# A two-layer decoder trunk on one core: the pacing of weight tiles that are split ahead of their use

## The chip, the cores and the metric

The kernel runs on one core of a Trainium2 chip. The metric is the device time of one execution in microseconds. The kernel before takes 1213.51 us, the median of three runs (1212.63 to 1216.22). Its profiled execution took 1216.67 us, of which the span from the first to the last instruction is 1214.9 us.

## The reference, cut to what matters

The input is 512 tokens of 1024 channels in float32. Two layers follow each other. Each normalises the input, projects it, runs four token mixers side by side, projects their outputs back and adds them. Then comes a feed-forward stage, and it is in the first layer's feed-forward stage that the change works:

```
h = rms_norm(x, ffn_norm[l])
g, up = jnp.split(h @ w_ffn_in[l], 2, axis=-1)      # 1024 -> 2 x 2816
x = x + (jax.nn.silu(g) * up) @ w_ffn_out[l]        # 2816 -> 1024
```

A last normalisation follows the second layer.

## The kernel before, in words

**Split products.** Every float32 matrix product is made of three matmuls in fp32r (`mm3`, L424). A weight tile of 128 x 512 numbers (256 KB) is loaded as `raw`. ScalarE (ACT) rounds it to `whi`, and VectorE (DVE), or now and then GpSimd (POOL), forms `wlo = raw - whi` (`load_split`, L522 to 532). Activations are split in the same way. TensorE (PE) then adds whi*xhi, whi*xlo and wlo*xhi into one PSUM tile. A weight tile holds four blocks of 128 columns, so it feeds 12 matmuls.

**The feed-forward stage** (L1191 to 1241). The 22 tiles of 128 hidden units are taken in two halves of 11. In a half, each hidden tile has a gate product and an up product (`dense_fm`, 24 matmuls each). DVE evicts them from PSUM as `fg` and `fu`, with the factor `rbc` of the normalisation. ACT applies silu to `fg`, DVE multiplies the two, and the result is split into `hsh` (ACT) and `hsl` (DVE or POOL). After 11 such tiles the half's output product follows: 8 output tiles of 33 matmuls each, added to `x` by DVE. So a half is 528 matmuls on `w_gu` and 264 on `w_fo`. In layer 0, 98 of the first 528 stand ahead of the small matmuls `ps_rbc` of the normalisation in PE's order; in layer 1 it is 95.

**Tiles split ahead.** During layer 0's feed-forward stage, the weights of layer 1's mixers are split ahead (`split_ahead`, L495). Such a tile is loaded as `praw`, ACT rounds it to `phi`, DVE or POOL forms `plo`, and both are written to device memory as `ahead`. When layer 1 needs the tile, it loads the two halves and casts nothing (L511 to 521). There are 64 such tiles, 54 of 256 KB and 10 of 128 KB. L1196 gives each of the 22 hidden tiles an equal share of them, and gates the share behind the last matmul of that hidden tile's gate product. The two output products get none.

**The order.** Nothing runs in the order of the source. Every instruction is recorded with an engine, a cost and a priority. A planner (`schedule`, L244) then plays a machine of five engines through and puts down each engine's instructions in the order in which it started them. Each engine executes its own list strictly in that order, and waits where an operand isn't there. Tiles split ahead have the lowest priority (60, `P_AHEAD`), evictions 2 and loads 1. At most two `praw` buffers and four `pre` buffers (`phi` and `plo`) exist at a time (`LIMIT`, L51).

**How the planner reckons a load.** L199 and L357 to 360: the DMA starts 0.7 us after the issuing instruction, which costs 0.48 us. It moves 360 GB/s, which makes 0.73 us for 256 KB, and its landing is seen 0.3 us later. So a 256 KB load with nothing ahead of it is reckoned to be there 2.2 us after its issue begins. All DMAs are issued by SyncE (SP), in its own list's order.

Of the kernel before, what the change touches and what calls it, by code (L numbers as in the profile page):

```python
# [23 lines left out]
KT = D // P  # L24
QT = S // P
HID = 2816
HT = HID // P
HH = HT // 2
# [80 lines left out]

class Op:  # L110
    __slots__ = ("i", "eng", "fn", "args", "kw", "cost", "tail", "table", "prio", "preds", "succs", "bufs", "news",
                 "left", "est", "far", "start", "end", "idle", "flex", "lock")


FLEXIBLE = ("tensor_sub", "tensor_mul", "tensor_add")
# [17 lines left out]
class Recorder:  # L133
# [55 lines left out]
    def add(self, eng, method, args, kw):  # L189
        op = Op()  # L190
        op.i = len(self.ops)
        op.eng, op.fn, op.args, op.kw = eng.name, getattr(eng.nc_engine, method), args, kw
        writes = [args[0]] + ([kw["accum_out"]] if "accum_out" in kw else [])
        writes = [w for w in writes if isinstance(w, View)]
        reads = [a for a in (*args[1:], *(v for k, v in kw.items() if k != "accum_out")) if isinstance(a, View)]
        views = writes + reads
        op.cost = self.cost(eng.name, method, args, kw, views) / self.share + self.extra
        op.tail = 0.0
        if method == "dma_start":  # L199
            op.tail = views[0].cols * 4 * P / 360.0  # L200
        op.flex = None
        if eng.name == "dve" and method in FLEXIBLE and not any(v.buf.cls == "psum" for v in views):
            op.flex = getattr(self.pool.nc_engine, method), self.cost("pool", method, args, kw, views)
        op.lock = (method in ("tensor_sub", "tensor_mul", "tensor_add") and eng.name == "pool" and "op" not in kw
                   or eng.name == "dve" and method not in ("memset", "reciprocal")
                   and not any(v.buf.cls == "psum" for v in views))
        op.idle = 0.0
        if method == "matmul":
            l, r = args[1:3]
            op.idle = op.cost - (4 if r.dtype == F32 else 1) * r.cols / 2.4 * (l.p[1] - l.p[0]) / P  # L210
        op.table = TABLES.get(args[2]) if method == "activation" else None
        op.prio = self.prio
        preds = set(self.gate)
        op.bufs = []
        for vs, w in ((writes, True), (reads, False)):
            for v in vs:
                b = v.buf
                if b not in op.bufs:
                    op.bufs.append(b)
                if b.cls == "psum":  # L220
                    if b.log:
                        preds.add(b.log[-1])
                    b.log = [op.i]
                    continue
                p0, p1, m = v.region()
                keep = []
                for e in b.log:
                    j, jw, q0, q1, k = e
                    hit = p0 < q1 and q0 < p1 and (m & k)
                    if hit and (w or jw) and j != op.i:  # L230
                        preds.add(j)
                    if not (w and hit and p0 <= q0 and q1 <= p1 and (m & k) == k and j != op.i):
                        keep.append(e)
                keep.append((op.i, w, p0, p1, m))
                b.log = keep
        preds.discard(op.i)
        op.bufs += [v.buf for v in self.also if v.buf not in op.bufs]
        for b in op.bufs:
            b.uses += 1
        op.preds, op.succs = preds, []  # L240
        self.ops.append(op)
        return op

    def schedule(self):  # L244
# [49 lines left out]
        while done < len(ops):  # L294
# [8 lines left out]
            for e in engines:  # L303
                fu, re = future[e], ready[e]
                while fu and fu[0][0] <= t:
                    _, i = heapq.heappop(fu)
                    heapq.heappush(re, (ops[i].prio, i))
                if busy[e] > t or not re:
                    continue
                skipped, pick = [], None  # L310
                while re:
                    c = heapq.heappop(re)
                    op = ops[c[1]]
                    if op.start is not None:
                        continue
                    if e == "pool" and op.flex and busy["dve"] + SPILL * len(ready["dve"]) < t + op.flex[1]:
                        skipped.append(c)
                        continue
                    if e == "pe":
                        late = op.prio > -5.0 and (t < op.far or (op.idle > 0.4 * op.cost and cool > COOL)) and (re or skipped)  # L320
                    else:
                        late = e == "act" and op.table not in (None, table) and t - op.est < 5000.0 and (re or skipped)
                    if not late and place(op):
                        pick = op
                        break
                    skipped.append(c)
                    if len(skipped) > 60:
                        break
                if pick is None and e in ("pe", "act"):
                    for c in skipped:  # L330
                        if place(ops[c[1]]):
                            pick = ops[c[1]]
                            skipped.remove(c)
                            break
                for c in skipped:
                    heapq.heappush(re, c)
                if pick is None:
                    continue
                op = pick
                if e != op.eng:  # L340
                    op.eng, (op.fn, op.cost) = e, op.flex
                cost = op.cost * (2 if e == "pe" and t < WARM else 1 if e == "pe" else CARE)
                if op.table and op.table != table:
                    cost += 1300.0
                    table = op.table
                if e == "pe":
                    cool = max(0.0, cool + op.idle + t - busy[e] - 0.5 * (cost - op.idle))
                if op.lock:
                    other = held["pool" if e == "dve" else "dve"]
                    cost = max(cost, other - t + cost - 145.0)  # L350
                    held[e] = t + cost
                op.start, op.end = t, t + cost
                busy[e] = op.end
                order.append(op)
                done += 1
                moved = True
                if op.tail:  # L357
                    dma = max(dma, op.end + 700.0) + op.tail
                    op.tail = dma + 300.0 - op.end
                fin = op.end + op.tail  # L360
                for b in op.bufs:
                    b.uses -= 1
                    if not b.uses:
                        heapq.heappush(frees, (fin + RELEASE, op.i, b.n, b))
                for j in op.succs:
                    s = ops[j]
                    lat = LATENCY[e][s.eng] + (0.0 if s.eng == e else SLACK if s.eng == "pe" else SPARE)
                    s.est = max(s.est, fin + lat)
                    if s.eng != e:
                        s.far = max(s.far, fin + lat)  # L370
                    s.left -= 1
                    if not s.left:
                        heapq.heappush(future[s.eng], (s.est, s.i))
                        if s.flex:
                            heapq.heappush(future["pool"], (s.est, s.i))
# [25 lines left out]
def trunk_kernel(ctx: ExitStack, tc: tile.TileContext, io):  # L401
    nc = tc.nc
    R = Recorder(nc)
# [91 lines left out]
    def split_ahead(key, ap):  # L495

        n = ap.shape[-1]
        raw = t512("praw", F32, "praw", (n,))
        sp.dma_start(raw, ap)
        hi, lo = t512("pre", F32R, "phi", (n,)), t512("pre", F32R, "plo", (n,))  # L500
        with also(lo):
            act.copy(hi, raw)
# [616 lines left out]
    for l in range(L):  # L1119
# [68 lines left out]
        fnrm = nrm  # L1188
        last = l == L - 1
        later = [] if last else mixer_weights(l + 1)  # L1190
        for half in range(2):  # L1191
            hs = []
            for m in range(half * HH, (half + 1) * HH):
                pg = dense_fm(io["w_gu"][l, m, 0], fnrm)
                with prio(P_AHEAD), gate(R.ops[-1]):
                    for key, ap in later[m * len(later) // HT:(m + 1) * len(later) // HT]:  # L1196
                        split_ahead(key, ap)
                g = scaled(pg, fnrm, "fg", group="h")
                pu = dense_fm(io["w_gu"][l, m, 1], fnrm)
                with prio(P_EVICT):  # L1200
# [9 lines left out]
            with prio(P_DENSE):  # L1210
                w = Weights(io["w_fo"][l, half])
                for m in range(KT - tail):
                    ps = psum("d", "pd")
                    for k in range(HH):
                        end = mm3(ps, w.block(m * HH + k), hs[k], k == 0, k == HH - 1)
                    if m < KT - 1:
                        turn["w"] = end
                    with prio(P_NORM):
# [131 lines left out]
```

## Time and profile before

| | |
|---|---|
| median of three runs | 1213.51 us |
| profiled execution | 1216.67 us |
| its span | 1214.9 us |
| PE busy | 1176.7 us, 97% of the span |
| DVE, ACT, POOL busy | 57%, 44%, 18% |
| DMA moved | 175.26 MB, mean 144 GB/s |

All arithmetic stands on L397 of the profile, which is the line that emits the planned instructions. So the rows are told apart by the names of their tiles, not by lines. The stages of layer 0's feed-forward lie between 242 and 625 us, those of layer 1 between 842 and 1206 us. Matmuls are pipelined: each is shown some 390 ns long, and the next one starts some 227 ns after it.

### The profile page before, as it was taken

Reading aid. Unit: us, or ns where it says so; the run is one execution under the profiler, and the core shown is the slowest. Engines: PE = TensorE matmul, PEld = TensorE weight load, DVE = VectorE, ACT = ScalarE, POOL = GpSimd, SP = SyncE. Lnnn points to the kernel's source line nnn. Section 1 sums busy time; section 2 is a strip of 40 time slices with the busy share of each in tenths; the row PEclk is TensorE's granted clock in tenths of the full one; section 3 lists DMA queues with packets and bytes.
Section 4 is the critical chain, followed back from the end, with each engine's and each line's share of the span. In section 5 each row is a group of like instructions: output and inputs, shape, how many; then the busy total and the mean of one; then the engine's idle time right before and its main releaser. Section 6 shows DMA issues by size and latency. Waiting matters only on the chain.

```text
span 1214.9 us, 16334 instructions
## 1 busy us (share of the span) xinstructions
PE 1176.7 (97%) x5552; PEld 963.5 (79%) x5552; DVE 686.5 (57%) x1270; ACT 532.2 (44%) x971; POOL 219.1 (18%) x208
## 2 busy tenths in 40 slices
PE   8999989999989999989999999999999999999996
PEld 6778768788767888767888787888888888888886
DVE  7668778777555355455433575587544533544433
ACT  5546967554433234344323348555333322333331
POOL 5423453272000000000112312204300000000010
PEclk9999989999999999999999999999999999999998
DMA  6312132268877357777476423643333333222312
GB/s 204 118 44 74 54 113 70 69 217 295 260 256 232 100 185 268 236 237 244 140 215 216 126 86 119 229 137 121 104 96 98 99 99 96 96 96 96 102 55 70
DMA packets 101651, 175.26 MB, mean 144 GB/s; under 512 B 11328, under 2 KB 21952, under 8 KB 101568
## 3 DMA queue, kind: packets, MB, share of 16 engines
q1 hardware_dynamic: 101568, 174.22, 45.0%
q8 instruction: 44, 0.72, 0.2%
q14 instruction: 39, 0.32, 0.1%
HBM read 139.04 MB, written 35.13 MB: 143 GB/s over the span
## 4 chain that ended last, share of the span: by engine, by line
PE 58%; DMA 7%; DVE 1%; ACT 1%; issue 1%; SPq 1%; POOL 0%; DVEq 0%; ACTq 0%; POOLq 0%
PE pd L397 49%; PE pt L397 4%; DMA praw<-w_outa 3%; DMA praw<-w_tm 2%; PE ps_s L397 1%; DMA ahead<-phi 1%; ACT phi L397 1%; PE ps_o L397 1%; PE ps_pt L397 1%; SPq L397 1%; DMA praw<-w_outb 1%; DMA ahead<-plo 1%; PE ps_q L397 0%; PE ps_og L397 0%; DVE plo L397 0%
## 5 line engine op out<-in xcount | busy, mean ns | idle before, releaser
L397 PE MATMUL pd<-xhi,whi 128*128 128x512 f32 x896 | 351.5, 394 | 14.3 <-DVE fg L397 6.6
L397 PE MATMUL pd<-xhi,wlo 128*128 128x512 f32 x896 | 350.5, 393 | 0.7 <-POOL wlo L397 0.7
L397 PE MATMUL pd<-xlo,whi 128*128 128x512 f32 x896 | 351.1, 393 | 0.0
L397 ACT CAST whi<-raw 128x512 fp32r<-128x512 f32 (+2 forms) x330 | 200.9, 612 | 327.9 <-PE pd L397 283.8
L397 DVE TENSOR_TENSOR wlo<-raw,whi 128x512 fp32r<-128x512 f32 (+1 forms) x276 | 201.6, 733 | 163.4 <-ACT whi L397 150.8
L397 PEld LDWEIGHTS pd<-xhi,whi 128*128 128x128 f32 x896 | 168.6, 188 | 54.9 <-ACT whi L397 15.4
L397 PEld LDWEIGHTS pd<-xhi,wlo 128*128 128x128 f32 x896 | 168.1, 188 | 36.7 <-POOL wlo L397 1.7
L397 PEld LDWEIGHTS pd<-xlo,whi 128*128 128x128 f32 x896 | 168.7, 188 | 35.0 <-issue 1.4
L397 PE MATMUL pd<-hsh,whi 128*128 128x512 f32 (+1 forms) x374 | 142.1, 380 | 4.6 <-ACT hsh L397 4.1
L397 PE MATMUL pd<-hsl,whi 128*128 128x512 f32 (+1 forms) x374 | 141.8, 379 | 0.3 <-DVE hsl L397 0.3
L397 PE MATMUL pd<-hsh,wlo 128*128 128x512 f32 (+1 forms) x374 | 141.5, 378 | 0.0
L397 POOL TENSOR_TENSOR wlo<-raw,whi 128x512 fp32r<-128x512 f32 (+2 forms) x54 | 69.7, 1292 | 303.3 <-ACT whi L397 287.3
L397 POOL TENSOR_TENSOR sq<-sq 128x512 f32<-128x512 f32 x35 | 51.1, 1459 | 375.1 <-ACT sq L397 367.4
L397 PEld LDWEIGHTS pd<-hsh,whi 128*128 128x128 f32 x374 | 70.8, 189 | 18.7 <-ACT hsh L397 4.9
L397 DVE TENSOR_TENSOR plo<-praw,phi 128x512 fp32r<-128x512 f32 (+1 forms) x53 | 36.6, 693 | 80.9 <-ACT phi L397 80.9
L397 ACT CAST phi<-praw 128x512 fp32r<-128x512 f32 (+1 forms) x64 | 37.4, 587 | 102.2 <-DMA praw<-w_tm 23.0
L397 PEld LDWEIGHTS pd<-hsl,whi 128*128 128x128 f32 x374 | 70.7, 189 | 14.0 <-DVE hsl L397 1.0
L397 PEld LDWEIGHTS pd<-hsh,wlo 128*128 128x128 f32 x374 | 70.7, 189 | 12.8
L397 DVE TENSOR_TENSOR x<-x,pd 128x512 f32<-128x512 f32 (+1 forms) x66 | 43.3, 669 | 54.2 <-PE pd L397 54.1
L397 PE MATMUL pt<-whi,xlo 128*128 128x512 f32 x128 | 51.0, 398 | 0.0
L397 PE MATMUL pt<-whi,xhi 128*128 128x512 f32 x128 | 50.7, 396 | 0.0
L397 PE MATMUL pt<-wlo,xhi 128*128 128x512 f32 x128 | 50.6, 396 | 0.0
(259 smaller groups left out, 1523.9 us busy)
## 6 DMA issues: line engine op xcount, KB each, us to landing
raw<-w_gu SPq DMA_DIRECT2D x176, 256.0 KB, 2.6
raw<-w_fo SPq DMA_DIRECT2D x88, 256.0 KB, 2.7
ahead<-phi SPq DMA_DIRECT2D x54, 256.0 KB, 2.6
ahead<-plo SPq DMA_DIRECT2D x54, 256.0 KB, 3.4
whi<-ahead SPq DMA_DIRECT2D x54, 256.0 KB, 2.7
wlo<-ahead SPq DMA_DIRECT2D x54, 256.0 KB, 3.1
x<-xT SPq DMA_DIRECT2D x16, 256.0 KB, 5.4
raw<-w_fm SPq DMA_DIRECT2D x16, 256.0 KB, 2.6
```

The lines of the kernel that those rows point to most:

```text
L397: op.fn(*[r(a) for a in op.args], **{k: r(v) for k, v in op.kw.items()})
```

## The change

It has two parts. First, the 64 tiles are paced by matmuls done, over both gate-up halves and both output products. `pace(n)` is called after each gate product (n = 16) and after each output tile (n = 11). It releases tiles until the share released equals the share of the stage's 528 block steps that are behind. Second, the planner reckons that what waits for a `praw` load gets it 3.5 us later than before (`slow`). The reckoned occupancy of the DMA engines is not changed, and neither are other loads or the writes of `ahead`.

```
-        op.tail = 0.0
+        op.tail, op.slow = 0.0, 0.0
...
-                    op.tail = dma + 300.0 - op.end
+                    op.tail = dma + 300.0 + op.slow - op.end
...
-        sp.dma_start(raw, ap)
+        sp.dma_start(raw, ap).slow = 3500.0
...
+        total, paced = len(later), [0]
+        def pace(n):
+            paced[0] += n
+            with prio(P_AHEAD), gate(R.ops[-1]):
+                while later and (total - len(later)) * HT * 3 * KT < paced[0] * total:
+                    split_ahead(*later.pop(0))
...
-                with prio(P_AHEAD), gate(R.ops[-1]):
-                    for key, ap in later[m * len(later) // HT:(m + 1) * len(later) // HT]:
-                        split_ahead(key, ap)
+                pace(2 * KT)
...
+                    pace(HH)
```

PE's list is the same before and after, instruction by instruction. What moves stands on the other engines.

**Place 1.** ACT's list at the silu of the first half's tenth hidden tile (`fg_3861` before, `fg_3792` after). The number behind a name tells buffers apart. Before:

```order
L397 CAST phi_3774<-praw_3750 128x512
L397 CAST whi_3780<-raw_3725 128x512
L397 CAST phi_3788<-praw_3759 128x512
L397 CAST whi_3805<-raw_3744 128x512
L397 CAST hsh_3828<-fu_3808 128x512
L397 CAST whi_3833<-raw_3769 128x512
L397 CAST phi_3843<-praw_3816 128x512
L397 CAST whi_3856<-raw_3803 128x512
L397 ACTIVATE fg_3861<-fg_3861 128x512
```

and after:

```order
L397 CAST whi_3719<-raw_3667 128x512
L397 CAST whi_3740<-raw_3689 128x512
L397 CAST phi_3746<-praw_3699 128x512
L397 CAST phi_3753<-praw_3703 128x512
L397 CAST hsh_3761<-fu_3738 128x512
L397 CAST whi_3768<-raw_3713 128x512
L397 CAST whi_3794<-raw_3731 128x512
L397 ACTIVATE fg_3792<-fg_3792 128x512
```

Before, `phi_3843` is the last cast but one ahead of the silu, and it stands ahead of the cast of `raw_3803`, a load that SP issued before `praw_3816`. After, the `phi` casts come in pairs, four `whi` casts apart, and `phi_3746` stands behind the cast of `raw_3689`, the last load that SP issued before `praw_3699`.

**Place 2.** DVE's list at the eviction of the same gate product, before:

```order
L397 TENSOR_TENSOR hsl_3837<-fu_3808,hsh_3828 128x512
L397 TENSOR_TENSOR wlo_3834<-raw_3769,whi_3833 128x512
L397 TENSOR_TENSOR plo_3844<-praw_3816,phi_3843 128x512
L397 TENSOR_TENSOR fg_3861<-pd_3800,rbc_3036 128x512
L397 TENSOR_TENSOR wlo_3857<-raw_3803,whi_3856 128x512
```

and after:

```order
L397 TENSOR_TENSOR wlo_3741<-raw_3689,whi_3740 128x512
L397 TENSOR_TENSOR plo_3747<-praw_3699,phi_3746 128x512
L397 TENSOR_TENSOR hsl_3775<-fu_3738,hsh_3761 128x512
L397 TENSOR_TENSOR wlo_3769<-raw_3713,whi_3768 128x512
L397 TENSOR_TENSOR fg_3792<-pd_3735,rbc_3032 128x512
```

Before, the eviction stands directly behind a `plo`. After, two instructions stand between them, and the pair's second `plo` is POOL's.

**Place 3.** DVE's list at the end of the stage, where the next normalisation's factor is formed (`v`, `t`, `r`, then `rbc`), before:

```order
L397 TENSOR_SCALAR v_6169<-ps_ssq_6155 128x4
L397 SCALAR_TENSOR_TENSOR t_6180<-y_6173 128x4
L397 TENSOR_TENSOR t_6180<-t_6180,v_6169 128x4
L397 SCALAR_TENSOR_TENSOR r_6187<-t_6180,y_6173 128x4
L397 COPY rbc_6201<-ps_rbc_6194 128x512
```

and after:

```order
L397 TENSOR_SCALAR v_6159<-ps_ssq_6143 128x4
L397 TENSOR_TENSOR plo_6157<-praw_6088,phi_6156 128x512
L397 SCALAR_TENSOR_TENSOR t_6173<-y_6163 128x4
L397 TENSOR_TENSOR t_6173<-t_6173,v_6159 128x4
L397 SCALAR_TENSOR_TENSOR r_6183<-t_6173,y_6163 128x4
L397 TENSOR_TENSOR plo_6180<-praw_6109,phi_6179 128x512
L397 COPY rbc_6200<-ps_rbc_6191 128x512
```

The last two tiles split ahead now stand inside that chain. On SP, their loads stand among the first loads of layer 1's weights.

## Rows read from the trace of the kernel before

**Rows 1.** The page, part 1: busy time of the engines.

```profile
PE 1176.7 (97%) x5552; PEld 963.5 (79%) x5552; DVE 686.5 (57%) x1270; ACT 532.2 (44%) x971; POOL 219.1 (18%) x208
```

**Rows 2.** Busy time by stretch: stretch, length, engines, granted clock, DMA share, GB/s.

```profile
265.00:310.00 45.00, 45.00 (x200) 37.08 (x199) 32.16 (x42) 22.84 (x39) 11.01 (x8) 1.00 0.87 287
310.00:390.00 80.00, 71.71 (x309) 57.39 (x308) 44.90 (x66) 31.84 (x56) 3.32 (x3) 1.00 0.81 262
390.00:450.00 60.00, 60.00 (x266) 49.72 (x266) 23.89 (x36) 16.16 (x27) 0.00 (x0) 1.00 0.40 125
490.00:590.00 100.00, 91.35 (x386) 72.57 (x386) 52.96 (x82) 40.99 (x75) 6.92 (x8) 0.98 0.70 225
...
265.00:625.00 360.00, 343.06 (x1489) 278.80 (x1488) 193.71 (x280) 141.73 (x246) 30.05 (x25) 1.00 0.70 224
1023.00:1142.00 119.00, 119.00 (x527) 98.56 (x526) 58.18 (x86) 40.62 (x65) 0.00 (x0) 1.00 0.31 97
```

**Rows 3.** PE's waits, 250 to 640 us: total, times, longest.

```profile
PE pd L397 <- DVE fg L397: 7.1, 6, 2.1
PE pd L397 <- DVE fu L397: 5.4, 7, 1.1
```

**Rows 4.** Timeline of PE at the stages' borders: start, length, instruction.

```profile
264.88 0.47 PE L397 MATMUL pd<-xhi,wlo 128*128 128x512 f32 x1
560.74 0.47 PE L397 MATMUL pd<-hsh,whi 128*128 128x512 f32 x1 [0.55 <-DVE fg L397]
624.94 0.39 PE L397 MATMUL pd<-xhi,whi 128*128 128x512 f32 x1
864.76 0.47 PE L397 MATMUL pd<-xhi,wlo 128*128 128x512 f32 x1
1142.55 0.39 PE L397 MATMUL pd<-hsh,whi 128*128 128x512 f32 x1
```

**Rows 5.** Timeline of one PE wait, 351 to 360 us, by engine.

```profile
351.40 0.41 SPq L397 DMA_DIRECT2D praw<-w_fm  x1
...
357.11 0.62 ACT L397 CAST phi<-praw 128x512 fp32r<-128x512 f32 x1 [3.41 <-DMA praw<-w_fm]
...
357.76 0.69 DVE L397 TENSOR_TENSOR plo<-praw,phi 128x512 fp32r<-128x512 f32 x1 [3.25 <-ACT phi L397]
358.37 0.68 DVE L397 TENSOR_TENSOR fg<-pd,rbc 128x512 f32<-128x512 f32 x1
...
359.20 0.47 PE L397 MATMUL pd<-xhi,whi 128*128 128x512 f32 x1 [2.09 <-DVE fg L397]
```

**Rows 6.** ACT's waits, 265 to 625 us, and the landing of `praw`.

```profile
ACT phi L397 <- DMA praw<-w_tm: 23.0, 13, 3.8
ACT phi L397 <- DMA praw<-w_outa: 21.8, 10, 3.3
ACT phi L397 <- DMA praw<-w_fm: 19.0, 11, 3.4
ACT phi L397 <- DMA ahead<-phi: 11.9, 3, 5.2
...
DMA to landing us min/median/max: 2.2/4.0/5.6
```

**Rows 7.** Timeline at the end of layer 0's feed-forward stage: DVE and PE.

```profile
632.84 0.16 DVE L397 SCALAR_TENSOR_TENSOR t<-y 128x4 f32<-128x4 f32 x1 [1.13 <-POOL y L397]
...
633.24 0.16 DVE L397 SCALAR_TENSOR_TENSOR r<-t,y 128x4 f32<-128x4 f32 x1
...
634.65 0.60 PE L397 MATMUL ps_rbc<-cst,r 128*128 128x128 f32 x4
...
646.44 0.69 DVE L397 TENSOR_TENSOR kr<-pd,rbc 128x512 f32<-128x512 f32 x1 [10.46 <-PE pd L397]
```

**Rows 8.** Timeline of DVE and POOL at 338 us.

```profile
338.02 1.28 POOL L397 TENSOR_TENSOR wlo<-raw,whi 128x512 fp32r<-128x512 f32 x1 [25.11 <-ACT whi L397]
...
338.06 1.80 DVE L397 TENSOR_TENSOR fu<-fg,fu 128x512 f32<-128x512 f32 x1
```

More of the change, by code (lines that the diff above doesn't have):

```diff
@@ L111 @@
     __slots__ = ("i", "eng", "fn", "args", "kw", "cost", "tail", "table", "prio", "preds", "succs", "bufs", "news",
-                 "left", "est", "far", "start", "end", "idle", "flex", "lock")
+                 "left", "est", "far", "start", "end", "idle", "flex", "lock", "slow")
 FLEXIBLE = ("tensor_sub", "tensor_mul", "tensor_add")
```

## The prediction

> **What bounds the kernel now.** I read the page's busy times first, and PE leads with 97% [rows 1]. So only what PE waits for, or what slows it, can be won; DVE at 57% and ACT at 44% matter only where PE waits for them. Next I read busy time by stretch [rows 2]. The reader is to see two stretches of layer 0's feed-forward stage where PE isn't full: 310 to 390 us has 71.71 us of PE in 80, and 490 to 590 us has 91.35 in 100. That is 8.29 + 8.65 = 16.9 us of idle PE. In both, the DMA engines move 225 to 262 GB/s. Between them, from 390 to 450 us, nothing is split ahead for most of the time (125 GB/s) and PE is full. Layer 1's stage does the same products with nothing split ahead, at 97 GB/s, and PE is full there.
>
> The stage's true excess is larger than the idle time, since a matmul after a gap starts a fresh pipeline and the clock fell once, so I take it from starts [rows 4]. Layer 1 goes from 864.76 to 1142.55 us with 433 + 264 + 528 = 1225 matmuls, so 277.79 / 1225 = 0.2268 us each. Layer 0's same part goes from 264.88 to 560.74 us, 295.86 us with 1222 matmuls, which at that pace would take 277.11: an excess of 18.75 us. Its last output product goes from 560.74 to 624.94 us, 64.20 us for 264 matmuls, against 59.87: an excess of 4.33. Together **23.1 us**. That is the most that this stage can give back. It includes the clock: of these stretches only 490 to 590 us, where PE waits most, has a granted clock under 1.00, namely 0.98 [rows 2]. With the two levels 1.2 and 2.4 GHz that is some 4 us at the lower one, and it costs half of that, about 2 us.
>
> Then I read who ends PE's waits: DVE's evictions `fg` and `fu`, 12.5 us in 13 waits [rows 3]. These take 0.68 us each, so the question is why they are late, and the timeline of the longest such wait answers it [rows 5]. SP issues a `praw` load at 351.40. ACT, which takes its list in order, sits 3.41 us before `phi` for that load, until 357.11, 5.7 us after the issue began. DVE sits 3.25 us for `phi`, does `plo`, and only then the eviction `fg` that stands behind it, at 358.37. PE has waited 2.09 us when it goes on at 359.20. A tile that nobody needs before layer 1, over 260 us later, holds up an eviction that PE needs now, because the planner put both in one list with the load reckoned there 2.2 us after its issue. Measured, it is there after a median of 4.0 us, at most 5.6 [rows 6].
>
> **The change, part by part.**
>
> The later landing. 58 of the 64 `phi` casts stood ahead of the cast of a `raw` that SP had issued before their own load, and 63 now stand behind it (place 1 shows one of each). Casts of `raw` follow each other every 12 matmuls, 12 x 0.2268 = 2.72 us, so most `phi` now stand at least that much later against their load. ACT's three largest groups of waits for `praw` are 23.0 + 21.8 + 19.0 = 63.8 us in 34 waits, 1.9 us each, 3.8 the longest [rows 6]. A mean wait is covered by 2.72 us, and of the longest 1.1 us would be left. At 359 us the wait was 3.41, and the eviction now has two instructions between it and the `plo` (place 2). So the waits for `praw` go, to within a little.
>
> The spread. Loads of `praw` stood 26, 6, 26, 6 in the four pieces of SP's list (gate-up, output, gate-up, output), and stand 19, 9, 22, 14 now. The stage's bytes are unchanged: 224 GB/s x 360 us = 80.6 MB [rows 2]. In 337 us (360 - 23) that makes 239 GB/s throughout, below the 287 GB/s at which PE ran full from 265 to 310 us. So I charge nothing for the busier output products, 390 to 450 us. If that cover failed, the price would be that of the bad stretches, which the rival below works out.
>
> What stays. The planner's new figure is for `praw` alone. ACT also waits for writes of earlier `phi` halves to land before it may reuse a buffer: 11.9 us in 3 waits [rows 6]. That is 11.9 / (63.8 + 11.9) = 16% of these waits. I let that share of the excess stay: 0.16 x 23.1 = 3.6 us. From below, the bound is zero, since fewer bytes per us bring the writes in sooner. From above, let every wait for `praw` be as long as the longest and leave 1.1 of 3.8 us, 29% of the rest: 3.6 + 0.29 x 19.5 = 9.3 us. I keep 3.6, being nearest to the rows of writes.
>
> POOL. Counted in the lists, it has 29 tensor operations in this stage, 25 before [rows 2]; beside one, a DVE operation took 1.80 instead of 0.69 us [rows 8]. Four more could cost DVE 4 x 1.1 = 4.4 us, if each fell on an eviction. DVE is busy 193.71 of 360 us here [rows 2], and that stretched `fu` ended at 339.86, with no PE wait ended by it. I take zero, and keep 4.4 as the end. The Trainium skill, "SBUF — State Buffer", section "SBUF: two separate sides", has a rule against this: a GpSimd operation and a VectorE operation with two SBUF inputs lock each other out of a shared port for the whole instruction. The stretched `fu` agrees with it in kind; by that rule with no slack, the sum below would be 4.4 us worse.
>
> The end of the stage. The last four tiles now load among layer 1's first weights, and two `plo` stand in the chain of the normalisation (place 3). SP issues their two loads ahead of the last write of `x`, so by about 626 us (the last output matmul before 624.94 [rows 4], its 0.39 us and an eviction of 0.7); with the longest landing, 5.6 us, they are there by 631.6. The first `plo`, 0.69 us, fits into the 1.13 us that `t` waited for POOL [rows 7]. Then `r` ends as before, at 633.40, and PE takes it up at 634.65: 1.25 us of cover. `rbc`, behind the second `plo`, is needed at 646.44, some 11 us later. I charge zero. If they come 5.2 us late, the longest wait in the rows, 5.2 - 1.25 = 4.0 us show.
>
> The sum: -23.1 + 3.6 = **-19.5 us**. Against the profiled execution, 1216.67 - 19.5 = 1197.2 us. That execution lay 3.16 us above the median of the three runs; against the median it is 1194.0. If part of that distance was more waiting in this very stage, the truth lies between, and I take the middle, **1195.5 us**.
>
> **The rivals.**
>
> Half stays. The new distance is one `raw` cast, not more, and pairs of `praw` followed at once by two or three `raw` loads land in a queue. For it: the longest landing is 5.6 us, and writes aren't reckoned later. Against it: the mean wait is 1.9 us. With half of 23.1 us left, 1213.5 - 11.6 = 1202 us.
>
> The change doesn't do what it says. Waits re-form elsewhere in the same amount, for instance at `raw` loads that SP now issues behind the writes. Against it: ACT's three largest waits name `praw`, not `raw`. The time would be 1213 us.
>
> Slower: waiting goes with the time in which tiles are split ahead, not with crowding. Then 23.1 us came from 310 to 390 and 490 to 590 us, 180 us, 0.128 us of loss per us. Spread over the stage's 337 us that makes 43 us, 20 more than now: 1234 us. It decides only where more than the present 23.1 us is lost, that is above 0.069 us per us, at 0.54 of the old rate. For it: a tile still puts a cast on ACT and a subtraction on DVE or POOL in front of evictions. Against it: from 265 to 310 us tiles were split ahead at 287 GB/s with no loss.
>
> **How the numbers follow.** The forecast has 0.70, half stays 0.18, the same waits elsewhere 0.06, slower 0.06. The low end is the median less the whole excess, 1213.5 - 23.1 = 1190.4, and no row speaks for less. The high end takes the upper bound of what stays (9.3) and the median's distance (3.2): 1216.67 - 23.1 + 9.3 = 1202.9, and 3 us more for one of POOL's or the end's prices shown: 1206. That leaves out the last two cases and a little of the second. A measurement of this kernel tells 0.3% (3.6 us) from no change, so faster means below 1209.9. The forecast and nearly all of the second case lie there: 0.88. Same 0.07, slower 0.05.
>
> **What would show it.** PE full, or within 1 us per 20, in every stretch from 310 to 590 us; from the matmul after `ps_rbc` to the first output matmul of the second half 277 to 283 us instead of 295.86; ACT's waits for `praw` below 15 us; PE's waits for `fg` and `fu` below 3 us; no stretch at the lower clock after 240 us until the end; DMA near 240 GB/s in the output products. I am wrong if ACT's waits for `praw` stay above 30 us, if PE waits for `whi` or `wlo` instead, or if gaps show at 625 to 660 us.

## The result: 1192.55 us, and the profile after

The changed kernel took **1192.55 us** (median of four runs, 1191.97 to 1195.28), the kernel before 1214.6 us (median of four). The ratio is **0.9824** with a 95% interval of 0.9801 to 0.9846. The profiled execution took 1192.72 us, 23.95 us less than that of before. The forecast was 1195.5 us.

The page's first part, to be held against [rows 1]:

```profile
PE 1171.1 (98%) x5552; PEld 963.9 (81%) x5552; DVE 690.9 (58%) x1266; ACT 534.8 (45%) x971; POOL 228.5 (19%) x212
```

The work of all engines is the same to within a few operations. So what was won was waiting, and PE's slower pace behind its waits (its busy time fell by 5.6 us for the same matmuls). Busy time by stretch (stretch, length, engines with their counts, granted clock, DMA share, GB/s), against [rows 2]:

```profile
265.00:310.00 45.00, 45.00 (x200) 37.26 (x199) 32.56 (x43) 23.22 (x39) 8.70 (x6) 1.00 0.76 255
310.00:390.00 80.00, 80.00 (x355) 66.24 (x354) 43.79 (x65) 31.28 (x54) 5.14 (x4) 1.00 0.69 224
390.00:450.00 60.00, 60.00 (x267) 49.67 (x266) 31.31 (x47) 22.91 (x38) 2.64 (x2) 1.00 0.73 243
490.00:590.00 100.00, 100.00 (x443) 82.81 (x442) 58.45 (x77) 43.32 (x76) 21.71 (x16) 1.00 0.68 217
265.00:605.00 340.00, 339.70 (x1499) 280.96 (x1498) 197.38 (x274) 144.44 (x246) 42.29 (x31) 1.00 0.71 235
605.00:625.00 20.00, 20.00 (x94) 16.35 (x93) 4.77 (x10) 1.24 (x2) 1.63 (x2) 1.00 1.02 363
```

PE, the first column after the length, is now full in every stretch (0.3 us short of it from 265 to 605), also in the two where it stood at 71.71 of 80 and 91.35 of 100. The first output product (390 to 450) now carries 243 GB/s where it carried 125. The last row is new: as layer 1 begins, the DMA engines are busy throughout, at 363 GB/s.

PE's waits from 250 to 640 us, against [rows 3], are a single line, and ACT's from 265 to 602 us, against [rows 6], have no `praw` in them (total, times, longest):

```profile
PE pd L397 <- DMA wlo<-ahead: 0.3, 1, 0.3
```

```profile
ACT whi L397 <- PE pd L397: 164.4, 105, 2.6
ACT hsh L397 <- DVE fu L397: 6.9, 13, 1.7
ACT whi L397 <- DMA raw<-w_fo: 5.5, 4, 1.9
...
ACT phi L397 <- DMA ahead<-plo: 0.5, 2, 0.3
```

ACT now waits chiefly for PE: a `whi` cast needs a buffer that PE must first be done with, so ACT has done all that it may and idles until PE frees one. That is the row in which its **spare time** is read, and the experiments below turn on it.

PE's timeline at the borders, against [rows 4], in order of time:

```profile
263.74 0.47 PE L397 MATMUL pd<-xhi,wlo 128*128 128x512 f32 x1
...
540.85 0.39 PE L397 MATMUL pd<-hsh,whi 128*128 128x512 f32 x1
...
600.69 0.39 PE L397 MATMUL pd<-xhi,whi 128*128 128x512 f32 x1
```

From 263.74 to 540.85 are 277.11 us, to the hundredth what 1222 matmuls cost at layer 1's pace. From there to 600.69 are 59.84 (64.20 before). So the stage went from 295.86 + 64.20 = 360.06 us to 336.95, 23.11 less. It also begins 1.14 us earlier (263.74 against 264.88), for which no cause was looked for, and PE waits 0.3 us behind it: 23.11 + 1.14 - 0.3 = 23.95, the whole difference of the two executions.

How a tile split ahead passes now is seen in the timeline of SP (issues), in that of ACT, and in [rows 5] for the same before:

```profile
333.67 1.08 SPq L397 DMA_DIRECT2D praw<-w_tm  x2
...
335.71 3.05 SPq L397 DMA_DIRECT2D raw<-w_gu  x2
```

```profile
334.33 0.62 ACT L397 CAST whi<-raw 128x512 fp32r<-128x512 f32 x1 [2.05 <-PE pd L397]
335.11 0.64 ACT L397 ACTIVATE fg<-fg 128x512 f32<-128x512 f32 x1 [0.15 <-DVE fg L397]
337.05 0.62 ACT L397 CAST whi<-raw 128x512 fp32r<-128x512 f32 x1 [1.31 <-PE pd L397]
339.77 0.62 ACT L397 CAST whi<-raw 128x512 fp32r<-128x512 f32 x1 [2.10 <-PE pd L397]
340.30 1.14 ACT L397 CAST phi<-praw 128x512 fp32r<-128x512 f32 x2
```

Two `praw` loads are issued from 333.67 on. ACT does three `whi` casts and a silu meanwhile, and takes up both `phi` at 340.30, 6.6 us after the issue, without a wait (no brackets). Before, it stood at the `phi` 3.41 us and began it 5.7 us after the issue. The loads themselves land no sooner than before (2.2/4.0/5.6 us, [rows 6]):

```profile
DMA to landing us min/median/max: 2.6/3.9/5.8
```

### The profile page after: what moved, and what is told of

The parts are those of the page before. It is cut to its first block, busy times and chain, and to the rows that moved or that the text cites. A ratio compares the mean times of both kernels' runs of the same rounds, so it can differ in the third digit from the quotient of the medians.

```text
span 1190.9 us, 16295 instructions
## 1 busy us (share of the span) xinstructions
PE 1171.1 (98%) x5552; PEld 963.9 (81%) x5552; DVE 690.9 (58%) x1266; ACT 534.8 (45%) x971; POOL 228.5 (19%) x212
## 4 chain that ended last, share of the span: by engine, by line
PE 95%; DVE 1%; DMA 1%; issue 1%; ACT 1%; SPq 0%; POOL 0%; POOLq 0%; DVEq 0%; ACTq 0%
PE pd L397 77%; PE pt L397 8%; PE ps_s L397 2%; PE ps_o L397 2%; PE ps_pt L397 1%; PE ps_q L397 1%; PE ps_og L397 1%; DMA raw<-w_fo 1%; PE ps_g L397 1%; PE ps_d L397 0%; DMA x<-xT 0%; DMA wlo<-ahead 0%; SPq L397 0%; DVE out L397 0%; DVE plo L397 0%
## 5 line engine op out<-in xcount | busy, mean ns | idle before, releaser
L397 DVE TENSOR_TENSOR wlo<-raw,whi 128x512 fp32r<-128x512 f32 (+1 forms) x280 | 208.2, 746 | 190.3 <-ACT whi L397 175.3
L397 POOL TENSOR_TENSOR wlo<-raw,whi 128x512 fp32r<-128x512 f32 (+2 forms) x50 | 64.5, 1292 | 148.1 <-ACT whi L397 122.9
L397 DVE TENSOR_TENSOR x<-x,pd 128x512 f32<-128x512 f32 (+1 forms) x66 | 43.5, 669 | 48.8 <-PE pd L397 48.7
L397 POOL TENSOR_TENSOR plo<-praw,phi 128x512 fp32r<-128x512 f32 (+1 forms) x15 | 19.7, 1315 | 250.8 <-ACT phi L397 137.1
L397 DVE TENSOR_TENSOR fu<-pd,rbc 128x512 f32<-128x512 f32 x44 | 30.4, 691 | 51.8 <-PE pd L397 51.8
L397 DVE TENSOR_TENSOR fg<-pd,rbc 128x512 f32<-128x512 f32 x44 | 30.4, 691 | 42.8 <-PE pd L397 39.5
```

Source lines behind the costliest of these rows:

```text
L397: op.fn(*[r(a) for a in op.args], **{k: r(v) for k, v in op.kw.items()})
```

## The experiments

Two theories stood at the start. **A**, the prediction's: `phi` casts stand too early behind their loads in ACT's list, and the later landing cures that. **B**: the tiles are too crowded in the gate-up halves, and the spread cures it. A third, **C**, on the end of the stage, came out of the first run. "Loss" below is what the stage takes above 277.11 + 59.84 us, and 23.1 us before, 1.6 us of it at the lower clock. Each loss and each wait is read from one execution, the profiled one; the times are medians.

**1. The spread alone** (spread_early). The change without its line at L499:

```
-        sp.dma_start(raw, ap).slow = 3500.0
+        sp.dma_start(raw, ap)
```

> The even pacing alone: the planner reckons a praw load as early as before. In its lists 57 of 64 phi casts stand ahead of the cast of a raw load that was issued before their own load, as in the kernel before (58), while the praw loads stand 18, 10, 22, 14 over the four pieces (gate-up, output, gate-up, output), as in the changed kernel. Theory A (ACT and DVE execute their lists in order, and a phi that stands too early for its load holds up what stands behind it): ACT still waits for praw in some 50 places, 60 us or more in sum, and PE's part of the stage from the matmul after ps_rbc to the first output matmul of the second half stays 5 us or more above 277 us; 1198 to 1212 us. Theory B (crowded DMA makes the loads late, and spreading cures it): that part is within 2 us of 277, ACT's waits for praw are under 20 us, 1192 to 1196 us.

Measured: 1200.16 us (1196.07 to 1201.89), ratio to before 0.9857 (0.9827 to 0.9886). By the time alone A would have come true, but by accident: in the stage it failed. The matmuls run from 265.06 to 542.17, 277.11 us and no loss, though 57 of 64 `phi` casts still stand ahead of an older `raw`. B has the stage right, but not its own sign: ACT waits 46.8 us for `praw` from 265 to 605 us, not under 20 (80.7 before), and the loads land after a median of 3.4 us (4.0 before). ACT's waits of 310 to 390 us, and three stretches:

```profile
ACT whi L397 <- PE pd L397: 27.7, 20, 2.1
...
ACT phi L397 <- DMA praw<-w_tm: 5.8, 5, 1.6
ACT phi L397 <- DMA praw<-w_uq: 5.4, 3, 2.8
```

```profile
310.00:390.00 80.00, 80.00 (x355) 66.28 (x354) 45.89 (x71) 32.15 (x55) 1.03 (x1) 1.00 0.72 228
600.00:605.00 5.00, 2.33 (x11) 1.66 (x10) 1.36 (x2) 1.77 (x3) 1.29 (x1) 1.00 0.98 339
605.00:612.50 7.50, 4.70 (x12) 3.40 (x13) 2.47 (x4) 2.26 (x4) 1.27 (x1) 0.54 0.93 324
```

ACT still waits 11.2 us for `praw` here, but has 27.7 us in which it waits for PE. The loss is now at the crossing into layer 1: two gaps of PE, and a granted clock of 0.54 behind them, that is, mostly the lower of the two levels. The gaps are 2.67 us, up to 604.85, and 2.80 us, up to 608.35. The records show the lower level from 605.6 to 612.4 us; of that, PE works from 608.35 on, 4.05 us at half speed, which cost 2.0. Together 7.5 us. The profiled execution, the slowest of its four, took 9.2 us longer than that of the change: 7.2 of these are the crossing (7.5 less the change's 0.3) and 1.3 lie ahead of the stage. SP's timeline shows how the loads come late:

```profile
595.56 2.05 SPq L397 DMA_DIRECT2D ahead<-phi  x2
...
599.11 1.08 SPq L397 DMA_DIRECT2D whi<-ahead  x2
...
602.22 0.33 SPq L397 DMA_DIRECT2D praw<-w_outb  x1
602.61 1.22 SPq L397 DMA_DIRECT2D wlo<-ahead  x2
```

```profile
SPq L397 <- ACT phi L397: 4.4, 2, 2.2
```

SP too takes its list in order. From 585 to 606 us it waits 4.4 us for `phi` casts whose writes stand in its list ahead of loads: 2.2 us up to 586.23, ahead of the stage's own last loads, and 2.2 us up to 595.56, ahead of layer 1's first. The first `wlo<-ahead` stands behind one more `praw` load and is issued at 602.61, after the output product has ended at 602.0; PE goes on with it at 608.35, 5.7 us later, with the DMA engines at 324 to 339 GB/s. How much the wait, the place in the list and the slow landing are each worth was not separated. So B was right on the stage's time and wrong in the total.

**2. The later landing, crowding kept** (crowded_late). The kernel before with L199, L359 and L499 of the change. The planner by itself then moves some loads into the output products (21, 11, 22, 10); with more buffers they stay at 26, 6, 26, 6, as before:

```
-LIMIT = {"raw": 5, "w": 12, "p": 4, "praw": 2, "pre": 4}
+LIMIT = {"raw": 5, "w": 12, "p": 4, "praw": 3, "pre": 6}
...
-        sp.dma_start(raw, ap)
+        sp.dma_start(raw, ap).slow = 3500.0
```

> The later landing alone, with the crowding kept: pacing as in the kernel before, 3.5 us more reckoned for praw, and three praw and six pre buffers instead of two and four, so that the later landing doesn't slow the tiles down. praw loads stand 26, 6, 26, 6 in the four pieces, just as before; all 64 phi casts stand behind the cast of every raw load issued before theirs; PE's list is that of the kernel before. Theory A: ACT's waits for praw fall below 15 us, PE's part is within 3 us of 277 us although the DMA engines move 260 GB/s and more in the same stretches; 1192 to 1197 us. Theory B: the loads land late as before, and at least half of the 23 us excess stays: 1204 to 1215 us.

Measured: 1193.87 us (1192.51 to 1194.98), ratio 0.9816 (0.9795 to 0.9837). B fell as well: with the old crowding, 1.45 us of loss are left. The crowded stretch, ACT's waits in it, and the landing of `praw`:

```profile
310.00:390.00 80.00, 78.99 (x349) 64.90 (x348) 46.50 (x73) 33.14 (x57) 1.37 (x2) 1.00 0.81 271
```

```profile
...
ACT phi L397 <- DMA ahead<-phi: 9.6, 5, 3.3
ACT whi L397 <- DMA raw<-w_fo: 9.1, 6, 3.3
ACT whi L397 <- PE pd L397: 8.2, 5, 2.1
ACT whi L397 <- DMA raw<-w_gu: 4.6, 5, 2.2
...
ACT phi L397 <- DMA praw<-w_tm: 1.2, 1, 1.2
```

```profile
DMA to landing us min/median/max: 2.5/4.3/6.3
```

The DMA engines move 271 GB/s, more than the 262 of before, the loads land later than before, and PE is nearly full. So neither bandwidth nor a sooner landing was what PE lacked: it is enough that the casts stand later. With run 1, either part of the change takes all or nearly all of the loss out of the stage. This run has more buffers besides; run 4 is the control for them, and run 3 goes without.

**3. The later landing alone** (late_alone). As 2, with the old `LIMIT`; loads 21, 11, 22, 10.

> The second part of the change alone: the old pacing by 22 hidden tiles, 3.5 us more reckoned for praw, two praw buffers. Since a buffer is held longer, the tiles fall behind their release and spread by themselves: praw loads stand 21, 11, 22, 10 in the four pieces. Theory A: all of the gain, 1191 to 1196 us, ACT's waits for praw under 15 us. Theory B: part of the gain, since the tiles are spread less evenly than in the change: 1196 to 1206 us.

Measured: 1195.25 us (1192.98 to 1196.19), ratio 0.9825 (0.9803 to 0.9847); the stage loses 1.73 us, and PE's only wait is one of 1.4. ACT's largest DMA wait, 265 to 605 us:

```profile
ACT phi L397 <- DMA ahead<-plo: 30.0, 12, 4.6
```

This is the prediction's "what stays": with `praw` reckoned later, the casts wait for the writes that free their buffers.

**4. The extra buffers alone** (buffers_alone). The control to 2: its `LIMIT`, without `slow`.

> The kernel before, with three `praw` and six `pre` buffers instead of two and four, and the planner's old landing. SP's list has 26, 6, 26, 6 `praw` loads in the four pieces, as before and as in crowded_late, and 59 of 64 `phi` casts stand ahead of the cast of the `raw` issued before their load (before 58, crowded_late none). It is crowded_late without its later landing. If the later landing was the cure there: the loss stays, 290 us or more from the matmul after ps_rbc to the second half's output product (277.1 without loss), ACT's waits for `praw` 60 us or more, time 1207 to 1218 us. Rival, if the extra buffers were the cure: stage 277 to 281 us, 1192 to 1198 us.

Measured: 1208.47 us (1203.2 to 1210.88), ratio 0.9916 (0.9888 to 0.9943). The time lies in the first range, but neither length of the stage held (285.1 us), and ACT waits 45.6 us for `praw`, not 60. The loss is 1.9 us at `ps_rbc`, just ahead of the stage, 8.0 up to the second output product and 5.9 in it, 15.8 in all, of which 4.9 are the lower clock (1.6 before). So the buffers give back a third, or half if the clock is left out. Run 2, with the later landing besides, was faster still: its ratio is 0.9816, each ratio with runs of before on its own chip, and the difference of 0.0100 is some 12 us. So the landing cures here, and the buffers help.

**5. A third of the later landing** (late_a_third). As 3, with `slow = 1200.0`; loads 26, 6, 26, 6.

> The kernel before with the later landing alone, 1.2 instead of 3.5 us later. 26, 6, 26, 6 `praw` loads; 44 of 64 `phi` casts stand ahead of the cast of the `raw` issued before their load (before 58, with 3.5 us hardly any). If PE loses only what exceeds ACT's spare time, waits shorter by a third to a half take away more than half of the loss: less than 8 us above 277.1 and the output product's 59.9 together, time 1195 to 1203 us. Rival, loss in proportion to the casts that stand ahead: 44/58 of 23 us stay, 17.5 us, time 1207 to 1212 us.

Measured: 1200.84 us (1199.75 to 1202.64), ratio 0.9858 (0.984 to 0.9876). The time is in the first range. The loss is 10.9 us (1225 matmuls stand behind `ps_rbc` here, three more than before), so more than half is gone, but not as much as I had said. It lies in the first half, where ACT still waits for `praw`, and now for writes:

```profile
310.00:390.00 80.00, 73.12 (x310) 58.59 (x309) 45.39 (x65) 31.01 (x55) 6.44 (x5) 0.98 0.77 260
```

```profile
ACT phi L397 <- DMA ahead<-phi: 16.7, 5, 4.8
ACT phi L397 <- DMA praw<-w_tm: 12.1, 6, 3.6
ACT phi L397 <- DMA praw<-w_fm: 10.3, 5, 2.6
ACT whi L397 <- PE pd L397: 7.2, 4, 2.1
```

**6. The subtraction on POOL** (plo_on_pool). The kernel before, with all `plo` off DVE's list:

```
-        dve.tensor_sub(lo, raw, f(hi))
+        pool.tensor_sub(lo, raw, f(hi))
```

> The kernel before with one thing changed: every plo is formed by POOL instead of DVE, so that DVE's list holds nothing that waits for a praw load. ACT's list still holds phi as early as before, and the crowding is the same (26, 6, 26, 6). Theory A: DVE's waits for phi go (80 us), its evictions fg and fu come sooner, and PE's waits for fg and fu fall from 12.5 us to under 6; ACT's waits for praw stay above 50 us, and hsh and silu still stand behind them, so PE's part comes down from 295.9 but not to 277: 282 to 291 us, and 1198 to 1208 us in all. Theory B: no change in the loads, PE's part stays above 292 us and the time within 4 us of before.

Measured: 1211.92 us (1208.24 to 1213.77), ratio 0.9957 (0.9944 to 0.9971). 20.0 of the 23.1 us stay (17.46 and 2.56), and PE's part is 294.6 us, as B said; the time is 4.7 us below before, a little more than B's 4. But the gaps and the clock have to be told apart. PE's waits fell from 16.9 to 11.8 us, those for `fg` and `fu` from 12.5 to 6.4, just short of A's mark. The clock fell three times in the stage, where before it fell once, and PE's 10.2 us at the lower level cost 5.1 instead of 1.6. POOL also became busy, 22.91 of 80 us in the crowded stretch against 3.32, and DVE's mean operation went from 0.68 to 0.81 us. So DVE's wait for the `plo` in front of the eviction, the one of [rows 5], is part of the loss, and more than half of PE's waits come without it. How much it would be worth without POOL's side effect, this run can't say.

**7. The cast on POOL too** (phi_plo_on_pool). As 6, with

```
-            act.copy(hi, raw)
+            pool.tensor_copy(hi, raw)
```

> The kernel before, with its crowded pacing (26, 6, 26, 6) and its early reckoning, but phi and plo are both formed by POOL, so that neither ACT's list nor DVE's holds anything that waits for a praw load. Theory A (what stands behind a late load in an engine's list is what costs): the stage's loss goes, PE's part is within 3 us of 277 us with 260 GB/s in the same stretches, POOL's waits for praw are long and cost nothing, 1192 to 1197 us. Theory B (crowding): the loss stays above 15 us, 1207 us or more. If POOL, at some 1.3 us for each of its 128 operations, can't keep up, the tiles run later than in before, and the end of the stage loses a little.

Measured: 1205.28 us (1203.02 to 1207.76), ratio 0.9918 (0.9897 to 0.9939), a loss of 13.5 us instead of none (1218 matmuls stand behind `ps_rbc` here). The waits of `phi` and `plo` for `praw` are now POOL's, which PE doesn't need, but a new loss came with them:

```profile
310.00:390.00 80.00, 74.11 (x320) 59.23 (x319) 48.02 (x53) 23.03 (x40) 38.58 (x37) 1.00 0.83 271
```

```profile
...
ACT fg L397 <- DVE fg L397: 42.9, 16, 4.3
ACT hsh L397 <- DVE fu L397: 37.6, 16, 4.1
ACT whi L397 <- DMA raw<-w_gu: 30.8, 20, 3.7
```

DVE takes 48.02 / 53 = 0.91 us per operation here, against 44.90 / 66 = 0.68 before [rows 2], with POOL busy 38.58 us instead of 3.32. It is not a mere mixture of other operations: from 265 to 600 us, `hsl` went from 0.78 to 1.13 us and `wlo` from 0.72 to 0.86, both with two inputs in SBUF, while the evictions `fg` and `fu`, which read one input from PSUM, stayed at 0.69. The Trainium skill, "SBUF — State Buffer", section "SBUF: two separate sides", has GpSimd and a VectorE operation with two SBUF inputs lock each other out of a shared port; the trace agrees in kind. ACT then waits for DVE (80.5 us over the stage), and for `raw` loads. How much of the 13.5 us each of the two is worth was not separated.

**8. The spread, done earlier** (early_done). Theory C: what spread_early lost, it lost because the last tiles are still being split when layer 1's loads begin. The spread alone, paced to end 44 of 528 block steps sooner:

```
-                while later and (total - len(later)) * HT * 3 * KT < paced[0] * total:
+                while later and (total - len(later)) * (HT * 3 * KT - 44) < paced[0] * total:
```

> spread_early with one more edit: the pacing ends 44 of its 528 steps before the stage does, so that no tile split ahead is left when layer 1's weights load. phi casts still stand as early as before (60 of 64 ahead of an older raw). Theory C (in spread_early the stage itself loses nothing, and its 8 us against the change come from the crossing into layer 1, where SP's list holds layer 1's loads behind writes that wait for phi, at 339 GB/s): PE's two waits of 2.7 and 2.8 us for whi and wlo of layer 1 and the lower clock after them go, 1190 to 1194 us, although ACT still waits 40 us or more for praw. Rival D (the early reckoning itself costs those 8 us, in waits that come out wherever PE's slack is least): 1197 to 1202 us.

Measured: 1194.47 us (1191.01 to 1198.85), ratio 0.9834 (0.981 to 0.9858). The median lies 0.5 us above C's range and below D's, and the interval overlaps that of spread_early, so the times alone don't show a gain. The trace shows what C said: PE's waits at the crossing fall from 5.5 to 1.1 us, SP's first `whi<-ahead` is out at 594.82 and its first `wlo<-ahead` at 597.69, and no lower clock follows. (In the change itself, executed twice, the crossing's wait was 0.3 and 1.6 us, so a difference of 4.4 is more than that.) The loads now stand 20, 11, 23, 10. ACT meanwhile waits for `praw` nearly as long as before:

```profile
ACT phi L397 <- DMA praw<-w_fm: 27.7, 11, 5.1
...
ACT phi L397 <- DMA praw<-w_outa: 18.7, 9, 3.1
ACT phi L397 <- DMA praw<-w_tm: 15.7, 8, 3.3
```

That is 62.1 us in these three groups, against 63.8 in [rows 6], and the stage loses 2.1 us instead of 23.1. So the sum of waits off the bounding engine does not tell the loss.

**9. The change, done earlier, and the change again** (change_done, change_again), the first with the line of 8.

> The changed kernel with the same early end of the pacing. Theory C: PE's wait at the crossing is already 0.3 us in the change, so within 2 us of it, with less DMA traffic between 605 and 625 us than 363 GB/s; Rival D: the same. If it is faster than the change by more than 0.3%, the crossing cost more than its waits show.

> The changed kernel once more, beside the others on the same chip: 1191 to 1196 us by every theory; PE's part from the matmul after ps_rbc to the first output matmul of the second half 277.1 us, the crossing's waits under 1 us.

Measured: 1192.62 us (1191.03 to 1193.5), ratio 0.9812 (0.9794 to 0.983), and 1195.25 us (1191.59 to 1197.17), ratio 0.9832 (0.981 to 0.9854). The two intervals overlap, so this is no shown gain (0.2% between the medians). With the earlier end PE has no wait at all from 250 to 640 us; without it one of 1.6 us for `wlo<-ahead`, above the 1 us that I had expected. From 605 to 625 us:

```profile
605.00:625.00 20.00, 20.00 (x95) 16.38 (x93) 3.39 (x8) 0.00 (x0) 1.02 (x1) 1.00 0.82 272
```

```profile
605.00:625.00 20.00, 20.00 (x95) 16.66 (x95) 4.34 (x10) 2.01 (x4) 2.31 (x2) 1.00 1.02 354
```

The first row is change_done's: 272 GB/s where the change has 354 and 363.

**What they say together.** ACT's time of waiting for PE (`whi`, its spare time) and PE's idle time, in the two stretches where the kernel before loses:

| run | spare, 310 to 390 us | PE idle of 80 | spare, 490 to 590 us | PE idle of 100 |
|---|---|---|---|---|
| plo_on_pool | 1.3 | 5.56 | 4.4 | 5.34 |
| phi_plo_on_pool | 2.1 | 5.89 | 8.4 | 4.12 |
| before | 4.6 | 8.29 | 5.3 | 8.65 |
| late_alone | 4.9 | 1.39 | 38.4 | 0 |
| late_a_third | 7.2 | 6.88 | 12.3 | 0.41 |
| crowded_late | 8.2 | 1.01 | 42.4 | 0 |
| buffers_alone | 11.8 | 3.01 | 13.8 | 2.93 |
| change_done | 26.3 | 0 | 44.6 | 0 |
| early_done | 26.9 | 0 | 1.4 | 0 |
| spread_early | 27.7 | 0 | 32.0 | 0 |
| the change | 46.2 | 0 | 48.8 | 0 |

With 26 us or more PE loses nothing, whatever ACT waits for. Less than that tells nothing by itself: late_alone, at 4.9, loses a sixth of what the kernel before loses at 4.6, and early_done, at 1.4 in the second stretch, loses nothing:

```profile
490.00:590.00 100.00, 100.00 (x442) 82.40 (x441) 56.07 (x84) 43.06 (x78) 12.47 (x11) 1.00 0.70 226
```

ACT waits 14.3 us for `praw` in that stretch, against 31.1 before. So much spare time is a sign that waits are harmless. That PE loses when it is used up was my reading, and it is not shown; in the first stretch, moreover, the four runs without loss are just those with the spread. The later landing's cure is shown by runs 2 and 4. Why the spread keeps PE full with 57 to 60 casts still early stays open: neither the landing (a median of 3.8 us in early_done) nor the sum of the waits (71.6 us there) explains it.

## Why the prediction was right

- **The 23.1 us of the stage**: right, 23.11 measured, clock included. No lower level shows between 240 us and the end's normalisation. The number is no test of how it was won, since either part of the change would have brought most of it.
- **The later landing**: right that it suffices to within 1.7 us (run 2 with more buffers, run 3 with tiles that spread by themselves), and that `praw` waits go. Not seen: it isn't needed in the stage, for the spread alone empties it as well (run 1). The reading of [rows 5] was right for that wait, but the `plo` ahead of an eviction is only part of the loss (run 6).
- **The spread, charged nothing**: the charge held. The DMA engines moved 235 GB/s over the stage (239 reckoned) and PE stayed full in the output products. But the step took the spread for a neutral edit, and it is a cure of its own. Without the later landing it also had a price in the one execution traced, 5.5 us of gaps and 2.0 of clock at the crossing, at a place where the prediction had looked at DVE's chain and not at SP's list.
- **What stays, 3.6 us**: the mis-sized term; in the change 0. The mechanism may be real: late_alone has 1.73 us of loss with 30.0 us of waits for writes. But its size can't be had from a share of waits: change_done has 20.2 us of such waits and loses nothing, and the change 0.5. Nor did the writes come in sooner, as the lower bound had it: those of `phi` landed after a median of 3.0 us, 2.5 before (265 to 600 us). Without this term the forecast would have been 1192.0 instead of 1195.5. The change executed again gave 1195.25, so the median of 1192.55 alone could not have told the two apart; the trace does.
- **POOL**: 212 operations instead of 208 on the page, and zero, as reckoned. Run 7 shows a price when POOL is busy half of the time.
- **The end of the stage**: 0.3 us at the crossing (1.6 when run again), inside the 4.0 kept for it, but of another kind: loads of `ahead`, at the highest DMA rate of the profile, not the normalisation.
- **The rivals**: that half stays, or the same waits elsewhere, is excluded by the single wait of 0.3 us. That the loss goes with the time of splitting is refuted: tiles are split all through 337 us and PE loses nothing.

Of the signs, all showed. Of those that would prove me wrong, one showed in small: PE's single wait is for `wlo`, 0.3 us, at the crossing. I named ACT's `praw` waits above 30 us as another; runs 1 and 8, with 46.8 and 71.6 us of them and a full or nearly full PE, show that this sign was badly chosen.

## What to carry to other kernels

An engine that takes its list in order holds up all that stands behind an operand not yet there, also what the bottleneck needs. So ask of every early load where its first use stands, not how soon it lands: in the kernel before they cost 23 us, and in the change, landing no sooner, nothing. A planner that reckons a load's landing too soon (2.2 us here, 4.0 measured) and work crowded into one stretch do harm together, and either can be mended. On an engine that isn't the bottleneck, the sum of its waits does not tell the harm. How long it waits for the bottleneck is a better sign, but in one direction only: with 26 us or more of it in a stretch no wait cost anything here, and with less some did and some didn't. Work that is spread to the end of a stage meets the next stage's first loads: look at the in-order issue queue there. Letting the spread end a little earlier took PE's waits at that crossing from 5.5 to 1.1 us in run 8; in the change itself it is no shown gain (run 9).

## What the runs showed of the hardware

- At the crossing of the change the DMA engines moved 363 GB/s over 20 us, and PE stayed full. The Trainium skill, "DMA: Bandwidth & Descriptors", section "Where 436 GB/s comes from", gives about 358 GB/s as what the memory side lets one core have; the 363 and 354 of two runs lie within 2% of it. That no more could be had, no run here shows.
- In late_a_third PE stood still for 2.2 us up to 346.81, and the granted clock stayed at its upper level. After 2.1 us up to 373.34 and 0.9 more up to 374.71 it was at the lower one from 375.9 to 379.3 us. In spread_early it fell at 605.6, after the gap up to 604.85, as the second one began.
- VectorE's mean operation went from 0.68 to 0.91 us with GpSimd busy half of the time beside it; its operations with two inputs in SBUF took longer, its evictions from PSUM did not.
- Loads of `praw`, most of them of 256 KB, landed after a median of 4.0 us (at most 5.6) in the kernel before, 3.9 (5.8) in the change, 3.4 (5.8) in spread_early and 4.3 (6.3) in crowded_late.
